# Cosine-similarity attention on one core: TensorE work cut into 64-row halves, joint operations on VectorE, four exponential chunks off ScalarE instead of two

## The chip, the cores and the metric

The kernel runs on one core of one Trainium2 chip. The metric is the device time of one execution in microseconds (us). A profile is one execution taken by the hardware profiler; its span runs from the first to the last instruction. The engines are TensorE (PE; its weight loads are listed apart as PEld), VectorE (DVE), ScalarE (ACT), GpSimd (POOL) and SyncE (SP), which here issues nearly all DMAs. Each engine works through its own list of instructions in order and waits for the others by semaphores.

## The reference

For 8 batches of 12 heads, 512 positions and 64 dimensions, in float32:

```python
Q_norm = Q / (np.linalg.norm(Q, axis=-1, keepdims=True) + 1e-10)
K_norm = K / (np.linalg.norm(K, axis=-1, keepdims=True) + 1e-10)
scores = np.einsum('bhqd,bhkd->bhqk', Q_norm, K_norm) / tau      # tau = 0.1
weights = np.exp(scores - np.max(scores, axis=-1, keepdims=True))
weights = weights / (np.sum(weights, axis=-1, keepdims=True) + 1e-10)
return np.einsum('bhqk,bhkd->bhqd', weights, V)
```

## The kernel before

The 96 heads are worked as 48 pairs `s` = 0 to 47 of two heads `h`. For each pair the kernel runs these operations; the short names are the keys that `P.add` gives them.

- `LD`, `LV`: DMA loads of Q (w = 0), K (w = 1) and V, 256 KB each (lines 318 to 325).
- `SQ`: squares of Q and K, from pair 4 on as one POOL instruction of 128x1024 (line 348); for pairs 2 and 3 two of 128x512 on POOL (line 342).
- `SSQ`, `RED`: sums of the squares. K's go through PE: eight matmuls of 64 columns against the identity, into columns 320 to 383 of an output bank (line 365), and then a reduction of 64 elements on DVE (line 372). Q's are reduced by DVE from 512 elements (line 376).
- `NEW`: reciprocal square roots by Newton steps on DVE (lines 401 to 410), done for groups of 1, 2 or 4 pairs.
- `SCL`: scaling of Q and K by them (line 434). Q on DVE; K on DVE for the pairs in `K_ON_DVE` and on POOL for the others.
- `TR`, `EVA`: eight PE transposes of 128x128 into `tps` (line 440), and the DVE copy from there to `qt` (line 455).
- `SCO`, `EXP`: for each of four chunks `c` of keys two PE matmuls with 64 rows and 512 columns, one for each head (line 552), and an exponential of 128x1024 on ACT (line 568). `scps` holds two chunks, so `SCO` of a chunk waits for the `EXP` two chunks earlier.
- A chunk in `OFF` gets its exponential as a polynomial: `SCX` on PE into `tps`, `X` on DVE (lines 502, 504), then `Y` steps on POOL and DVE (lines 509, 510).
- `VC`: V to bf16 on POOL (line 573).
- `PV`: 32 matmuls with 128 rows and 65 columns (line 585), one output bank for each head; `RCP` and `NRM` on DVE for each head apart (lines 604, 606); `ST`, the store.

Pair 0 has smaller forms of its own (`head0`), pair 47 others (`last`). The order of every engine is written out in `ORDER`: each number is the position at which `P.add` added the operation, so for one pair numbers run on. `run` turns needs between operations into semaphore waits; a wait stops its engine's whole list. On PE and ACT, needs on an operation of the same engine are dropped (lines 50 and 51), since these work in order. `HOLD` adds single waits by hand.

Where the numbers that matter below lie, with (pair, chunk): before the change 36 to 55 belong to the scores of pair 0, 83 and 85 are `TR` of pair 1, 87 is `SCO`(1,0), 89 (1,1), 91 (1,2), 93 (1,3); 132, 134, 136 and 138 are `SCO`(2,0) to (2,3); 159 and 161 are `SSQ` of pair 3 for Q and K; 203 is `SSQ` of pair 4, 246 of pair 5. POOL's list begins, in both kernels, with squares of pairs 0 to 3, `VC` of pairs 0 and 1, `SQ` of pair 4 and `SQ` of pair 5.

Of the kernel before, what the change touches and what calls it, by code (L numbers as in the profile page):

```python
# [5 lines left out]
ALU = mybir.AluOpType  # L6
# [4 lines left out]
class Op:  # L11
    def __init__(self, key, eng, kind, due, needs, emit, slot=None):
        self.key, self.eng, self.kind, self.due, self.emit = key, eng, kind, due, emit
        self.needs, self.slot = [n for n in needs if n is not None], slot
        self.own = False
        self.sem, self.val, self.inc, self.used = None, 0, 0, False
        self.start = self.end = None


class Program:  # L20
# [22 lines left out]
    def run(self):  # L43
# [3 lines left out]
        for e, ops in order.items():  # L47
            for o in ops:
                o.waits = [self.ops[n] for n in o.needs]
                if e in ("pe", "act") and not o.own:  # L50
                    o.waits = [p for p in o.waits if p.eng != e or p.slot is not None]
                for p in o.waits:
                    p.used = True
# [55 lines left out]
def bass_cosine_similarity_attention_kernel(  # L109
# [10 lines left out]
    NT = SEQ // 128  # L120
# [85 lines left out]
    slots = sorted((START + PERIOD * (s + 1) + 0.9 * PV_AT[4 * h + 3] + 0.05 + late(s), s, h) for s in range(NP - 1) for h in range(2) if s not in PV_LATER)  # L206
# [8 lines left out]
    session, attached, early = {}, {}, []  # L215
    for s, w in sorted(((s, w) for s in range(NP) for w in range(2) if on_pe(s, w)), key=lambda j: (due_red(j[0]), j)):
        at = due_red(s) + 0.3
        if s < EARLY:
            early.append((s, w))
            continue  # L220
        due, i, h = next(x for x in slots if x[0] >= at and (x[1], x[2]) not in attached)
        attached[i, h] = (s, w)
        session[s, w] = (h, due, [("PV", i, h, NT - 1)])
    before = [[("EVA", 0, 1, 0), ("EVA", 0, 1, 1)], []]
    for s, w in sorted(early):
        session[s, w] = (w, due_red(s), before[w])
        before[w] = [("RED", s, w)]
    bank_free = {}
    sequence = list(range(NP))
    for s, k in PV_LATER.items():  # L230
        sequence.remove(s)
        sequence.insert(s + k, s)
    for s in sequence:
        for h in range(2):
            bank_free[s, h] = before[h]
            before[h] = [("NRM", s, h)] + ([("RED",) + attached[s, h]] if (s, h) in attached else [])

    def head0(TF):
        for h in range(2):
# [4 lines left out]
            cast_in = qk[0][:, 1, h, :].rearrange("p (t d) -> p t d", t=NT)  # L244
# [6 lines left out]
            for w in range(2):  # L251
                src_, dst = qk[0][:, w, h, :], sq[0][:, 8 * w + 4 * h : 8 * w + 4 * h + 4, :]
# [3 lines left out]
                else:  # L256
# [12 lines left out]
                      out=qn[0][:, 0, :, h, :], in0=qk[0][:, 0, h, :].rearrange("p (t d) -> p t d", t=NT),  # L269
# [23 lines left out]
    def new(g):  # L293
        if g <= 0:
            return []
        return [("NEW", g, 7)] if direct_r(g) else [("NEW", g, 6), ("NEW", g, 7)]
# [7 lines left out]
    def last_direct(s):  # L304
        d = [g for g in NORM_ON_ACT if g > 0]
        return [("NEW", max(d), 7 if direct_r(max(d)) else 6)] if d and group[s] not in NORM_ON_ACT and s < 12 else []

    def pair(s):
# [6 lines left out]
        for w, x in ((0, Q), (1, K)):  # L315
            if s == 0:
                for h in range(2):
                    P.add(("LD", 0, w, h), "act" if w else "sp", "ldh", -1000 + h,  [],
                          lambda e, w=w, x=x, h=h: e.dma_start(out=qk[iq][:, w, h], in_=src(x, s)[:, h]), slot=f"head{w}_{h}")  # L319
                continue  # L320
            P.add(("LD", s, w), "act" if (s, w) in BY_SCALAR else "sp", "ld1" if s == 1 else "ld", s, [*([("CST", 0, i) if w else ("SCL", 0, 0, i) for i in range(2)] + [("SQ", 0, w, 0), ("SQ", 0, w, 1)] if s == R_QK else [key("SCL", s - R_QK, w), *(squares(s - R_QK, w) if s >= R_QK else [])])],
                  lambda e, w=w, x=x: e.dma_start(out=qk[iq][:, w], in_=src(x, s)),  # L322
# [6 lines left out]
        red = [[("RED", 0, w, 0), ("RED", 0, w, 1)] if s == R_SQ else [key("RED", s - R_SQ, w)] for w in range(2)]  # L329
# [3 lines left out]
        elif s in SQ_ON:  # L333
            for w, engs in enumerate(SQ_ON[s]):
                for h, eng in enumerate(engs if isinstance(engs, tuple) else (engs,)):
                    n = 1 if isinstance(engs, tuple) else 2
                    half = qk[iq][:, w, n * h : n * h + n].rearrange("p h x -> p (h x)")
                    dst = sq[iqs][:, 8 * w + 4 * h : 8 * w + 4 * h + 4 * n, :].rearrange("p g d -> p (g d)")
# [17 lines left out]
        x2 = (xs[g][:, 0 : 2 * m] if acts else n_ps[:, g % R_X, 0 : 2 * m]).rearrange("p (w x) -> p w x", w=2)  # L356
        for w in range(2):
            sqs = squares(s, w)
            dst = x2[:, w, c8 : c8 + 8]
            if (s, w) in session:  # L360
                bank, due, before = session[s, w]

                def ssq(e, w=w, bank=bank):
                    for k in range(8):
                        last = e.matmul(  # L365
                            out=o_ps[bank][:, 320:384], lhsT=ident[:, :], rhs=sq[iqs][:, 8 * w : 8 * w + 8, 8 * k : 8 * k + 8],
# [3 lines left out]
                P.add(("SSQ", s, w), "pe", "ssq", due, [*sqs, "eye"] + before, ssq)  # L370
                P.add(("RED", s, w), "dve", "redp", due + 0.1, [("SSQ", s, w), ("NRMS", 0, 0, 1), *new(g - R_X), *last_direct(s)],
                      lambda e, bank=bank, dst=dst: e.tensor_reduce(  # L372
                          out=dst, in_=o_ps[bank][:, 320:384].rearrange("p (g e) -> p g e", e=8), axis=AX.X, op=ALU.add))
            else:
                P.add(("RED", s, w), "dve", "red", due_red(s) + 0.5 * w, [*sqs, ("NRMS", 0, 0, 1), *new(g - R_X), *last_direct(s)],
                      lambda e, w=w, dst=dst: e.tensor_reduce(  # L376
                          out=dst, in_=sq[iqs][:, 8 * w : 8 * w + 8, :], axis=AX.X, op=ALU.add))
# [5 lines left out]
        on_dve = [i for i in range(first[g], first[g] + sizes[g]) if i in K_ON_DVE]  # L383
        free = [[("SCL", i, k) for i in range(first[g - R_X], first[g - R_X] + sizes[g - R_X])] if g > R_X else []
                for k in range(2)]
        reds = [("RED", i, w) for i in range(first[g], first[g] + sizes[g]) for w in range(2)]
# [13 lines left out]
        elif s == first[g]:  # L400
            yx = lambda e: e.tensor_tensor(out=tg, in0=xg, in1=yg, op=ALU.mult)  # L401
            yyx = lambda e: e.scalar_tensor_tensor(  # L402
                out=tg, in0=tg, scalar=-0.5, in1=yg, op0=ALU.mult, op1=ALU.mult)

            def up(dst, lo, hi):
                return lambda e: e.scalar_tensor_tensor(  # L406
                    out=dst, in0=tg[:, lo:hi], scalar=1.5, in1=yg[:, lo:hi], op0=ALU.add, op1=ALU.mult)
# [5 lines left out]
                yx, yyx, up(yg, 0, 2 * m), yx, yyx, up(rq_g, 0, m), up(rk_g, m, 2 * m)]  # L413
            if on_dve:
                steps.append(up(tg[:, m : 2 * m], m, 2 * m))
            for k, step in enumerate(steps):
                needs = [("NEW", g, min(k, 6) - 1 if k < 8 else 7)] if k else reds + (free[1] if K_ON_DVE else [])
                if k == 0 and g == R_X:
                    needs += [("NRMS", 0, w, h) for w in range(2) for h in range(2)]
                if 6 <= k < 8:  # L420
                    needs += free[k - 6]
                P.add(("NEW", g, k), "dve", "new", TF - 4.9 - slack(s, M_NEW) + (M_STEP * (k - 7) if s > 8 else 0.23 * k), needs, step)

        if s in off_of:
            P.add(("UNIT", s), "dve", "new", TF - 3.0, [("NEW", g, 6)], lambda e: e.tensor_scalar(
                out=rq_g[:, c8 : c8 + 8], in0=rq_g[:, c8 : c8 + 8], scalar1=UNIT * inv_tau / math.log(2.0), scalar2=1.0,
                op0=ALU.mult, op1=ALU.mult))
        for w in range(2):
            dve = w == 0 or s in K_ON_DVE
            r = (rkd[:, c8 : c8 + 8] if dve else rk_g[:, c8 : c8 + 8]) if w else rq_g[:, c8 : c8 + 8]  # L430
            r = r.rearrange("p (h t) -> p h t", h=2).unsqueeze(3).to_broadcast([128, 2, NT, DIM])
# [405 lines left out]
```

## Time and profile before

| | |
|---|---|
| device time, median of 3 runs | 188.92 us (188.57 to 189.04) |
| profiled execution | span 186.6 us; the page gives no other time of it; the median is 2.3 us above |
| busy share of the span | PE 94%, DVE 94%, ACT 97%, POOL 86% |
| DMA | 37.75 MB read, 12.58 MB written, 270 GB/s over the span |
| granted TensorE clock | 0.998 |

In the profile a group of instructions is listed with its line, engine, operation, output<-input, shapes and count, then the busy time and the mean of one in ns. A timeline row is: start, length, engine, line, operation, tiles, count, and in brackets the idle time before it with what ended it. A matmul's length holds its latency, so matmuls in a row overlap; what one costs its engine is the distance from start to start. The same holds, by a smaller amount, for DVE and ACT.

### The profile page before, as it was taken

What the parts mean: (1) busy time and instruction counts of PE and PEld (TensorE: products, weight loads), DVE (VectorE), ACT (ScalarE), POOL (GpSimd) and SP (SyncE); (2) the same over time, 40 slices, a digit from 0 to 9 for tenths busy, and PEclk for the clock granted to TensorE, in tenths of its full rate; (3) what the DMA queues carried; (4) which work ended last, traced back from release to release, by engine and by line L of the source; (5) the groups of instructions that cost most, each with busy time, mean ns of one, the idle gap of its engine ahead of it and who ended that gap; (6) DMA issues with size and microseconds to landing.
All of it is one profiled execution on the core that took longest, in us unless ns stands there. A gap on an engine that the chain in (4) does not pass through costs nothing.

```text
span 186.6 us, 6661 instructions
## 1 busy us (share of the span) xinstructions
PE 174.7 (94%) x2705; PEld 108.6 (58%) x2705; DVE 174.9 (94%) x567; ACT 181.1 (97%) x213; POOL 161.3 (86%) x148
## 2 busy tenths in 40 slices
PE   6998899999999999999999999899999999999993
PEld 2455466656666565656666565466655666555662
DVE  2799999999999999999999999999999999999863
ACT  5999999999999999999999999999999999999993
POOL 5689999999999999999999999977999999398000
PEclk9999999999999999999999999999999999999999
DMA  4999999999999999999999999999306221131535
GB/s 162 326 359 348 348 350 369 348 351 367 379 368 355 295 372 352 376 356 382 376 355 380 374 346 317 354 319 286 118 4 189 88 90 35 58 114 61 169 102 183
DMA packets 52446, 50.76 MB, mean 272 GB/s; under 512 B 3264, under 2 KB 52416, under 8 KB 52416
## 3 DMA queue, kind: packets, MB, share of 16 engines
q1 hardware_dynamic: 51984, 50.05, 80.4%
q8 instruction: 21, 0.34, 0.7%
q10 hardware_dynamic: 432, 0.30, 0.5%
q14 instruction: 9, 0.07, 0.1%
HBM read 37.75 MB, written 12.58 MB: 270 GB/s over the span
## 4 chain that ended last, share of the span: by engine, by line
ACT 88%; SPq 4%; DMA 4%; POOL 1%; DVE 1%; PE 1%; issue 0%
ACT et L568 88%; DMA qk<-in_K_dram 4%; SPq L322 2%; SPq L325 1%; POOL sq L348 1%; SPq L319 0%; DVE ob L640 0%; ACT et L563 0%; PE ops L365 0%; DVE rd L632 0%; PE scps L552 0%; PE ops L621 0%
## 5 line engine op out<-in xcount | busy, mean ns | idle before, releaser
L568 ACT ACTIVATE et<-scps 128x1024 bf16<-128x1024 f32 x185 | 170.0, 1201 | 0.2 <-PE scps L552 0.2
L348 POOL TENSOR_TENSOR sq<-qk 128x1024 bf16<-128x1024 f32 x44 | 82.6, 1892 | 1.4 <-DVE xz L510 1.3
L552 PE MATMUL scps<-qt 64*128 64x512 bf16 x372 | 72.6, 386 | 4.6 <-ACT et L568 2.4
L585 PE MATMUL ops<-vb,et 128*128 128x65 bf16 x1504 | 72.8, 194 | 0.9 <-DVE ob L606 0.4
L585 PEld LDWEIGHTS ops<-vb,et 128*128 128x128 bf16 x1504 | 55.2, 98 | 30.1 <-issue 17.8
L434 DVE TENSOR_TENSOR qn<-qk,nps 128x512 bf16<-128x512 f32 x61 | 40.4, 676 | 0.6 <-ACT nps L393 0.6
L606 DVE TENSOR_TENSOR ob<-ops,rd 128x256 f32<-128x256 f32 x94 | 38.5, 417 | 0.5
L434 POOL TENSOR_TENSOR qn<-qk,rk 128x512 bf16<-128x512 f32 x33 | 34.1, 1042 | 3.3 <-DVE rk L406 3.2
L440 PE MATMUL tps<-ident,qn 128*128 128x128 bf16 x376 | 33.3, 221 | 0.5 <-DVE qn L434 0.2
L455 DVE COPY qt<-tps 128x1024 bf16<-128x1024 bf16 x47 | 32.1, 682 | 0.2 <-PE tps L440 0.2
L376 DVE TENSOR_REDUCE nps<-sq 128x8 f32<-128x512 bf16 x46 | 30.4, 683 | 0.2
L573 POOL TENSOR_SCALAR vb<-vf 128x512 bf16<-128x512 f32 x48 | 29.2, 625 | 1.4 <-PE ops L585 1.3
L552 PEld LDWEIGHTS scps<-qt 64*128 64x128 bf16 x372 | 18.0, 93 | 21.0 <-ACT et L568 7.8
L440 PEld LDWEIGHTS tps<-ident,qn 128*128 128x128 bf16 x376 | 21.4, 98 | 13.3 <-issue 4.3
L365 PE MATMUL ops<-sq,ident 128*128 128x64 bf16 x384 | 18.9, 193 | 1.0 <-POOL sq L348 0.5
L604 DVE RECIPROCAL rd<-ops 128x4 f32<-128x4 f32 x94 | 15.5, 172 | 2.7 <-PE ops L585 2.6
L365 PEld LDWEIGHTS ops<-sq,ident 128*128 128x128 bf16 x384 | 14.2, 98 | 4.2 <-POOL sq L342 1.7
L372 DVE TENSOR_REDUCE nps<-ops 128x8 f32<-128x64 f32 x46 | 9.8, 215 | 0.0
L402 DVE SCALAR_TENSOR_TENSOR nps<-nps,ys 128x32 f32<-128x32 f32 (+2 forms) x34 | 7.0, 207 | 0.4
L401 DVE TENSOR_TENSOR nps<-nps,ys 128x32 f32<-128x32 f32 (+2 forms) x34 | 7.0, 206 | 0.4
L342 POOL TENSOR_TENSOR sq<-qk 128x512 bf16<-128x512 f32 (+1 forms) x5 | 4.7, 954 | 2.2 <-DMA qk<-in_K_dram 1.6
L192 PE MATMUL ops<-warm_in,ident 128*128 128x512 bf16 x8 | 3.6, 628 | 1.4 <-POOL eps L185 1.4
(67 smaller groups left out, 69.4 us busy)
## 6 DMA issues: line engine op xcount, KB each, us to landing
vf<-in_V_dram SPq DMA_DIRECT2D x48, 256.0 KB, 6.5
qk<-in_Q_dram SPq DMA_DIRECT2D x47, 256.0 KB, 5.6
qk<-in_K_dram SPq DMA_DIRECT2D x47, 256.0 KB, 6.6
out_dram<-ob SPq DMA_DIRECT2D x47, 256.0 KB, 5.1
qk<-in_Q_dram SPq DMA_DIRECT2D x2, 128.0 KB, 2.6
qk<-in_K_dram ACTq DMA_DIRECT2D x2, 128.0 KB, 2.8
out_dram<-ob SPq DMA_DIRECT2D x1, 128.0 KB, 1.9
out_dram<-ob SPq DMA_DIRECT2D x1, 96.0 KB, 1.7
```

The source lines that it names most:

```text
L348: lambda e: e.tensor_tensor(out=sqf, in0=data, in1=data, op=ALU.mult))
L365: last = e.matmul(out=o_ps[bank][:, 320:384], lhsT=ident[:, :], rhs=sq[iqs][:, 8 * w : 8 * w + 8, 8 * k : 8 * k + 8], start=(k == 0), stop ...
L376: lambda e, w=w, dst=dst: e.tensor_reduce(out=dst, in_=sq[iqs][:, 8 * w : 8 * w + 8, :], axis=AX.X, op=ALU.add))
L434: lambda e, w=w, r=r: e.tensor_tensor(out=qn[iqn][:, w].rearrange("p t h d -> p h t d"), in0=qk[iq][:, w].rearrange("p h (t d) -> p h t d" ...
L440: last = e.transpose(t_ps[:, w, t, :], qn[iqn][:, w, t].rearrange("p h d -> p (h d)"), ident[:, :])
L455: lambda e: e.tensor_copy(out=qt[iqt][:, :, :, :].rearrange("p w t x -> p (w t x)"), in_=t_ps[:, :, :, :].rearrange("p w t x -> p (w t x)")))
L552: last = e.matmul(out=sc_ps[:, 2 * b + h, :], lhsT=qt[iqt][64 * h : 64 * h + 64, 1, c, :], rhs=qt[iqt][64 * h : 64 * h + 64, 0, :, :], sta ...
L568: lambda e, c=c, b=b: e.activation(out=et[iet][:, c, :, :], in_=sc_ps[:, 2 * b : 2 * b + 2, :], func=ACT.Exp, scale=math.log(2.0) / UNIT i ...
L573: lambda e: e.tensor_scalar(out=vb[:, iq, :, :, 0:DIM].rearrange("p c h d -> p h c d"), in0=vf[iv][:, :, :].rearrange("p h (c d) -> p h c ...
L585: last = e.matmul(out=o_ps[h][:, 65 * t : 65 * t + 65], lhsT=et[iet][:, c, h, 128 * t : 128 * t + 128], rhs=vb[:, iq, c, h, :], start=(c = ...
L604: (lambda e, h=h, grid=grid: e.reciprocal(out=rd[io][:, h, :], in_=grid[:, :, DIM])))
L606: lambda e, h=k, grid=grid: e.tensor_tensor(out=ob[io][:, h], in0=grid[:, :, 0:DIM], in1=rd[io][:, h, :].unsqueeze(2).to_broadcast([128, N ...
```

## The change

It is one rewrite with four parts.

1. **PE in 64-row halves, from pair 4 on.** Every `PV`, `SSQ` and `TR` matmul of 128 rows becomes two of 64 rows. In `PV` and `SSQ` rows 0 to 63 and rows 64 to 127 alternate and go to different output banks: in turn 0 the lower rows work on head 0 while the upper work on head 1, in turn 1 the other way round. Turn 1 waits for the end of turn 0; such waits of PE on itself are listed in the new `hard`. Q's and K's squares are both summed on PE. `TR` runs all eight lower halves as one operation and then, after a wait, all eight upper halves. Pairs 1 to 3 and 47 keep the 128-row form.
2. **Joint operations on DVE.** One `SCL` of 128x1024 for Q and K, one `RCP` and one `NRM` for both heads, one `RED` for up to two pairs; POOL scales nothing any more. The group's Newton steps are seven, not eight or nine.
3. **Four chunks off ACT**, (15,3), (24,3), (33,3) and (42,3), all of form B (`Y` 0 to 2 on POOL, 3 and 4 on DVE), not (30,3) and (43,3).
4. **New orders** for all engines, other `GROUPS` and `HOLD`. The layout of `qk` changes from [Q/K][head] to [head][Q/K].

```diff
+    def phase(i, turn):
+        return bank_half[i] if turn else [("PV", i, 0, 0)]
...
+                def sums(e, turn=turn):
+                    for k in range(8):
+                        for r in (0, 1):
+                            h = r ^ turn
+                            last = e.matmul(
+                                out=o_ps[h][:, at : at + 64], lhsT=ident[64 * r : 64 * r + 64, :],
+                                rhs=sq[iqs][64 * r : 64 * r + 64, 8 * h : 8 * h + 8, 8 * k : 8 * k + 8],
+                                start=False, stop=(turn == 1 and k == 7), skip_group_check=True)
+                    return last
+
+                P.add(("SSQ", s, turn), "pe", "ssqh", due_red(s), [("SQ", s, 0), "eye"] + phase(i, turn), sums).hard = phase(i, turn) if turn else []
...
+            P.add(("SCL", s), "dve", "sclj", T0 - 2.55 - slack(s, M_SCL), [("NEW", g, 6)] + gone,
...
+            def half(e, r=w):
+                rows = slice(64 * r, 64 * r + 64)
+                for w in range(2):
+                    for t in range(NT):
+                        last = e.transpose(
+                            t_ps[:, w, t, rows], qn[iqn][rows, w, t].rearrange("p h d -> p (h d)"), ident[rows, rows])
+                return last
...
+        for turn in (0, 1):
+            for c in range(NT):
+                def pv(e, c=c, turn=turn):
+                    for t in range(NT):
+                        for r in (0, 1):
+                            h = r ^ turn
+                            last = e.matmul(
+                                out=o_ps[h][:, 65 * t : 65 * t + 65],
+                                lhsT=et[iet][64 * r : 64 * r + 64, c, h, 128 * t : 128 * t + 128], rhs=vb[64 * r : 64 * r + 64, iq, c, h, :],
+                                start=(turn == 0 and c == 0 and t == 0), stop=(turn == 1 and c == NT - 1), skip_group_check=True)
                     return last
...
+        P.add(("RCP", s), "dve", "rcpj", T0 + 2 * PERIOD, bank_full[s] + [key("NRM", s - R_O)],
...
-OFF = {(30,3):((30,30),'B'),(43,3):((43,43),'A')}
+OFF = {(15,3):((15,15),'B'),(24,3):((24,24),'B'),(33,3):((33,33),'B'),(42,3):((42,42),'B')}
-GROUPS = [1, 1, 1, 1, 2, 2, 2, 2, 2, 2, 2, 2, 4]
+GROUPS = [1, 1, 1, 1, 1, 2, 2, 2, 2, 4]
...
     "pe": (
-        "6 24 22 -256 38 44 48 36 76 78 40 46 52 114 50 42 116 83 85 54 159 87 161 89 57 58 59 91 128 130 93 63 60 "
-        "64 132 203 65 134 66 246 136 172 174 138 176 102 178 103 104 105 280 180 215 217 182 96 97 98 219 147 99 "
...
+        "6 24 22 -256 38 44 48 36 74 76 40 46 52 110 50 112 42 151 153 81 83 54 85 57 87 191 59 58 89 122 124 60 91 229 "
+        "126 64 230 61 62 63 192 128 163 165 130 94 132 96 97 266 95 167 267 100 99 98 101 169 202 171 203 135 173 136 "
```

In the new PE list 151 and 153 are `SSQ` of pair 3 for Q and K, 81 and 83 `TR` of pair 1, 54 the scores of the last chunk of pair 0, 85, 87, 89 and 91 `SCO`(1,0) to (1,3), 57 to 64 `PV` of pair 0 (turn 0: 57 to 60), 191 and 192 `SSQ` of pair 4, 229 and 230 of pair 5, 122 and 124 `TR` of pair 2, 126 and 128 `SCO`(2,0) and (2,1).

More of the change, by code (lines that the diff above doesn't have):

```diff
@@ L214, in bass_cosine_similarity_attention_kernel @@
         users.sort()
[L215 to L228, printed above, removed]
     sequence = list(range(NP))
@@ L382, in pair @@
         rkd = n_ps[:, g % R_X, 128 + m : 128 + 2 * m] if acts else tg[:, m : 2 * m]
[L383 to L386, printed above, removed]
+        free = [scl(i, k) for i in range(first[g - R_X], first[g - R_X] + sizes[g - R_X]) for k in range(2)] if g > R_X else []
+        reds = [("RED", i, *w) for i in range(first[g], first[g] + sizes[g]) for w in (((0,), (1,)) if i < EARLY else ((),)) if i < EARLY or i in red_of]
         if s == first[g] and g in NORM_ON_ACT:
@@ L672 @@
 JOINT = ()
-PV_LATER = {30:1}
+PV_LATER = {15:1,24:1,33:1,42:1}
 TURNED = range(0)
```

225 lines of the change are left out of this document (125 added, 100 removed), and 146 rows, old and new, of the table ORDER.

## The prediction

> **What bounds the kernel now.** I read the page's busy shares first, then the chain of waits that ended last, then the groups by line, and last the timelines of the head (6 to 20 us) and of a steady stretch. From the page and, for L502 and L510, from the groups with shapes kept apart:
>
> ```profile
> PE 174.7 (94%) x2705; PEld 108.6 (58%) x2705; DVE 174.9 (94%) x567; ACT 181.1 (97%) x213; POOL 161.3 (86%) x148
> ACT 88%; SPq 4%; DMA 4%; POOL 1%; DVE 1%; PE 1%; issue 0%
> L568 ACT ACTIVATE et<-scps 128x1024 bf16<-128x1024 f32 x185 | 170.0, 1201 | 0.2 <-PE scps L552 0.2
> L434 DVE TENSOR_TENSOR qn<-qk,nps 128x512 bf16<-128x512 f32 x61 | 40.4, 676 | 0.6 <-ACT nps L393 0.6
> L606 DVE TENSOR_TENSOR ob<-ops,rd 128x256 f32<-128x256 f32 x94 | 38.5, 417 | 0.5
> L434 POOL TENSOR_TENSOR qn<-qk,rk 128x512 bf16<-128x512 f32 x33 | 34.1, 1042 | 3.3 <-DVE rk L406 3.2
> L376 DVE TENSOR_REDUCE nps<-sq 128x8 f32<-128x512 bf16 x46 | 30.4, 683 | 0.2
> L455 DVE COPY qt<-tps 128x1024 bf16<-128x1024 bf16 x47 | 32.1, 682 | 0.2 <-PE tps L440 0.2
> L604 DVE RECIPROCAL rd<-ops 128x4 f32<-128x4 f32 x94 | 15.5, 172 | 2.7 <-PE ops L585 2.6
> L372 DVE TENSOR_REDUCE nps<-ops 128x8 f32<-128x64 f32 x46 | 9.8, 215 | 0.0
> L401 DVE TENSOR_TENSOR nps<-nps,ys 128x32 f32<-128x32 f32 (+2 forms) x34 | 7.0, 206 | 0.4
> L502 DVE TENSOR_SCALAR xp<-tps 128x512 int16<-128x512 f32 x4 | 2.7, 678 | 0.0
> L510 DVE SCALAR_TENSOR_TENSOR xz<-xz,xp 128x1024 f32<-128x1024 f32 x1 | 1.2, 1219 | 0.0
> ```
>
> PE and DVE look as full as ACT, but the chain is ACT's for 88%: its exponentials follow each other to the end. These rows give the pace, from the chain and from ACT's timeline in three windows:
>
> ```profile
> 15.32 1.90 POOL sq L348
> 18.04 164.34 ACT et L568 x179
> ...
> 85.95 2.94 ACT L568 ACTIVATE et<-scps 128x1024 bf16<-128x1024 f32 x3
> ...
> 98.60 3.11 ACT L568 ACTIVATE et<-scps 128x1024 bf16<-128x1024 f32 x3
> ...
> 181.96 1.47 ACT L563 ACTIVATE et<-scps 128x512 bf16<-128x512 f32 x3
> ```
>
> From 85.95 to 98.60 lie 14 chunks: 0.904 us each, a pair of four 3.62 us. From 18.04 to 181.96 the 179 chunks take 163.9 us where 179 x 0.904 is 161.8: **2.1 us are lost in small delays** of ACT. PE's steady timeline shows why:
>
> ```profile
> 100.26 0.40 PE L440 MATMUL tps<-ident,qn 128*128 128x128 bf16 x4
> 100.49 0.41 PE L585 MATMUL ops<-vb,et 128*128 128x65 bf16 x8
> 100.85 0.39 PE L552 MATMUL scps<-qt 64*128 64x512 bf16 x2
> 101.18 0.66 PE L585 MATMUL ops<-vb,et 128*128 128x65 bf16 x16
> 101.67 0.40 PE L365 MATMUL ops<-sq,ident 128*128 128x64 bf16 x8
> 102.00 0.39 PE L552 MATMUL scps<-qt 64*128 64x512 bf16 x2
> ...
> 6.49 0.60 PE L541 MATMUL scps<-qt 64*128 64x512 bf16 x2 [0.18 <-DVE qt L290]
> ```
>
> Matmuls for values start 0.031 us apart (16 in 0.49, from 101.18 to 101.67), sums about 0.03, transposes 0.058 (four in 0.23). Two score matmuls in the same 64 rows (L541) take 0.60, so one streams for 0.60 - 0.39 = 0.21. The two of L552, in different halves, take 0.39 together: **the halves run at the same time.** After them the next work starts not 0.21 but 0.33 later (100.85 to 101.18), and before them the last sum starts at 101.67 + 0.40 - 0.19 = 101.88, with the scores at 102.00 instead of 101.91. Each change of form costs about 0.1 us, eight changes a pair 0.8. PE's pair: scores 4 x 0.21, values 32 x 0.031, transposes 8 x 0.058, sums 8 x 0.03, changes 0.8, together 3.3 of 3.62 us. That leaves little; the chunk between 100.85 and 102.00 holds 1.15 us of PE work for 0.904 of ACT.
>
> **The change, part by part.**
>
> *Two more chunks off ACT.* 2 x 0.904 = **-1.8 us**, all on the chain.
>
> *PE in halves.* From pair 4 on nothing changes form. If alternating halves run like L552's, two of them cost one place: values 32 x 0.031, sums 16 x 0.03 (Q's are new), transposes 16 x 0.03 (64 columns, not 128, one half after the other), scores 0.84: 2.8 us a pair. A wait of PE for its own last matmul, 0.2 us (L365's length less a place), stands open where nothing lies between the turns, about once a pair, with the rest of the values and the next scores behind it; elsewhere scores or transposes lie between. So 3.0 us, and a chunk with four value operations and a sum is 24 x 0.03 + 0.21 = 0.93, against 1.15 above. This frees up to all of the 2.1 us (bounds 0 and -2.1, and a loss if halves do not pair up, below). I take half, **-1.0**, because DVE stays nearly full.
>
> *DVE.* Its timeline shows how much sooner than its length an instruction is followed:
>
> ```profile
> 105.16 0.68 DVE L434 TENSOR_TENSOR qn<-qk,nps 128x512 bf16<-128x512 f32 x1
> 105.75 0.18 DVE L604 RECIPROCAL rd<-ops 128x4 f32<-128x4 f32 x1
> 105.85 0.66 DVE L434 TENSOR_TENSOR qn<-qk,nps 128x512 bf16<-128x512 f32 x1
> ```
>
> By some 0.08 to 0.09: 676 ns cost 0.60. Before: L376 46 x 0.60, 42 of L372 x 0.13, L604 94 x 0.09, L606 94 x 0.34, L434 61 x 0.60. After: `SCL` 44 x 1.14 (L510's 1024 elements) and 6 x 0.60 (+17), `RED` 21 of 256 elements at 0.33 and two at 0.20 (-26), `RCP` 47 x 0.10 (-4), `NRM` 47 x 0.61 (-3), 37 fewer Newton steps and unit scalings at 0.12 (-4, by L401), four polynomials of 4 x 0.60 + 2 x 1.14 = 4.7 for two of 4.7 and 4.2 (+10). Sum -10 of about 170. Yet between pairs 13 and 42 a pair is 1.14 + 0.17 + 0.10 + 0.61 + 0.60 (L455) + 0.21 (Newton) = 2.83, and 30 x 2.83 + 19 = 104 us stand against ACT's 116 x 0.904 = 105: as full as before, hence only half of the delays.
>
> *POOL.* Loses 34 us of scaling, gains some 9 of polynomials; its squares run ahead of their use from pair 6 on, and I cost it at nothing. Without that cover DVE would stand at `Y` 3 for one POOL step, 1.9 us (15.32, as many elements), with copies for the next scores behind it: four times, 7.6 us at most. The new layout of `qk` keeps a load's runs at 256 floats, as the source has them: nothing, hidden behind the other loads of the queue.
>
> *The head.* Here the new order has a price. The timelines of POOL, ACT and PE before:
>
> ```profile
> 10.06 2.04 POOL L342 TENSOR_TENSOR sq<-qk 128x512 bf16<-128x512 f32 x2 [0.44 <-DMA qk<-in_Q_dram]
> 13.36 3.86 POOL L348 TENSOR_TENSOR sq<-qk 128x1024 bf16<-128x1024 f32 x2
> ...
> 8.76 3.56 ACT L544 ACTIVATE et<-scps,xs 128x512 bf16<-128x512 f32 x6
> 12.18 5.62 ACT L568 ACTIVATE et<-scps 128x1024 bf16<-128x1024 f32 x6
> 18.04 3.85 ACT L568 ACTIVATE et<-scps 128x1024 bf16<-128x1024 f32 x4 [0.24 <-PE scps L552]
> ...
> 10.05 0.68 PE L440 MATMUL tps<-ident,qn 128*128 128x128 bf16 x8
> 11.56 0.39 PE L552 MATMUL scps<-qt 64*128 64x512 bf16 x2
> 12.15 0.41 PE L365 MATMUL ops<-sq,ident 128*128 128x64 bf16 x8 [0.20 <-POOL sq L342]
> 17.61 0.39 PE L552 MATMUL scps<-qt 64*128 64x512 bf16 x2
> ```
>
> POOL's list and the loads up to pair 5 stay as they are, so pair 3's K squares end at 12.10, pair 4's at 15.25, pair 5's at 17.22, as now. Operation 153 (sums of 3, K) now stands ahead of `TR`(1), the last scores of pair 0 and `SCO`(1,0). It starts at 12.15, as the row shows; 8 x 0.03 gives 12.39, eight transposes 12.85, a change of form 12.95 for the scores of pair 0, and ACT follows 0.43 later (17.61 to 18.04) at 13.4 instead of 11.6 (8.76 + 5 x 0.57). `EVA`(1), behind the transposes' end at 13.0, takes 0.7 on DVE; `SCO`(1,0) goes at 13.75 instead of 11.56, `EXP`(1,0) at **14.2 instead of 12.18**. Next, 191 (sums of 4) stands ahead of `SCO`(1,2): 15.30, a sum operation 0.24, two of values 0.25, scores at 15.8, `EXP`(1,2) at **16.2 instead of 14.0**; not a second loss but the same one seen again. 229 (sums of 5) is ready at 17.27, with `EXP`(2,0) due at 18.1: in time. Between `SCO`(2,0) and (2,1) lie 32 places, 1.0 us, which makes `EXP`(2,1) 19.2, 0.2 late. From `EXP`(2,2), 20.1 against 18.04 (which holds the 0.24 of idle), ACT's pace decides up to pair 4, and nothing later gives it back, since ACT is full. **+2.0 us**; bounds 0 (if squares come sooner) and 2.7 (if the halves go singly: sum 0.47, values 0.5).
>
> *Tail.* Pair 47 keeps its forms; the joint `NRM` of 46 (0.7 us) ends before the last exponential: nothing.
>
> *Sum.* Span 186.6 - 1.8 - 1.0 + 2.0 = 185.8; the median lies 2.3 above the span: **188.0** (-0.5%). Own range: all delays gone 187.0, none gone and 0.2 more 189.3.
>
> **Rivals.**
>
> *Halves go singly (slower).* L552 shows two long matmuls side by side, but no row shows many short ones fed in a row; the closest, L585, needs a load and a matmul each 0.031 us. If that is the rate of the feed, PE's pair is 64 x 0.031 + 32 x 0.03 + 16 x 0.03 + 0.84 = 4.3, 0.65 over ACT's 3.62, for 43 pairs 28 us: about 216. At 0.04 for two places PE needs 3.4 with its waits, and it decides from about 0.044 for two; at 0.05 it is 3.9 and +12: 201; at 0.047, 195. The Trainium skill, page "TensorE: Matmul & The Clock Gate", section "Wait — 56ns, not 53.3ns?", has a floor of about 25 ns from start to start however small a matmul; by it, as an estimate, 112 short matmuls take 2.8 us and the pair 3.65 before waits, which is this rival at its mild end. L552's two, a few ns apart in a joint 0.39, speak against that floor across halves. For it: the feed of PE doubles, 240 loads and matmuls in 3.62 us. I give 0.27.
>
> *PE's relief buys nothing.* DVE sets the small delays, and the joint operations of 1.14 us hold up copies: 2.1 stays, 189.0 to 190. DVE's 94% speaks for it, the crowded chunk at 100.85 against. 0.14.
>
> *The head loses nothing.* 186.0 to 187.0, if loads of pairs 3 and 4 land 2 us sooner. The 0.44 us that POOL waited for Q at 10.06 says the transfers set it, and their order is unchanged. 0.07.
>
> *The change does not do what it says:* pairing fails to remove the changes of form, since transposes write 64 columns. Then PE needs 3.6 or more and it is the second rival again; its chance is within that.
>
> **How the numbers follow.** The forecast has 0.52: of it 0.38 faster by over 0.3% (under 188.35), 0.12 within, 0.02 slower. 0.3% is about what a measurement of this kernel can tell from no change. Head without loss 0.07, faster. PE's relief nothing: 0.06 within, 0.08 slower. Halves singly: 0.27 slower, half of it under 196. Together 0.45, 0.18, 0.37. The range 186.8 to 195 leaves out some 0.04 below and 0.15 above; the likeliest case alone is 187.0 to 189.3.
>
> **What would show it.** Right: ACT's first 128x1024 exponential near 14.2 with PE waiting for POOL's squares at 12.1 and 15.3; value matmuls in pairs a few ns apart, 0.03 from pair to pair; no gap of 0.1 around L552's successors; ACT at 0.904 in long stretches. Wrong: PE without idle and ACT waiting for scores in every pair (the halves go singly), an early start of pair 1, or DVE named before most late scores.

## The result and the profile after

| | before | after |
|---|---|---|
| device time, median | 188.75 us (188.42 to 189.04) | 230.99 us (228.55 to 235.05) |
| ratio | | 1.219 (95%: 1.213 to 1.226) |
| span of the profiled execution | 186.6 us | 228.8 us |
| granted TensorE clock | 0.998 | 0.921 |

Ratios rest on the fast runs alone: some executions of one program run some per cent longer, and the profiled execution of sums_turns_full (217.41 us), little_traffic (210.63) and before_split64_few (198.26) was such a slow one.

The change costs 42 us. The forecast was 188.0 us, the range ended at 195: direction and size were wrong. From the page of the changed kernel (busy rows, clock in 40 slices, DMA queues, chain, groups):

```profile
PE 178.0 (78%) x5633; PEld 129.8 (57%) x5633; DVE 170.2 (74%) x372; ACT 185.3 (81%) x211; POOL 137.3 (60%) x120
PEclk9958775979799999999979997999999999998898
q8 instruction: 44, 0.72, 1.4%
PE 47%; ACT 21%; issue 14%; DVE 11%; DMA 3%; SPq 1%; POOL 1%
L623 ACT ACTIVATE et<-scps 128x1024 bf16<-128x1024 f32 x183 | 173.8, 1041 | 35.5 <-PE scps L607 34.6
```

Of the page before, the one row that matters beside the prediction's is the queue that carries instructions:

```profile
q8 instruction: 21, 0.34, 0.7%
```

No engine is full any more. ACT waits 35.5 us ahead of its large exponentials (0.2 before), for scores; PE is busy for 78% only, and a new word stands in the chain with 14%: "issue", time in which an engine waited for nothing that the profile shows. The waits say where (us in all, times, longest):

```profile
ACT et L623 <- PE scps L607: 34.6, 38, 3.1
...
PEld ops L641 <- issue: 26.4, 37, 3.0
...
PE ops L641 <- issue: 18.0, 13, 2.9
```

PE's timeline in a steady stretch shows two such stops:

```profile
100.65 0.54 PE L641 MATMUL ops<-vb,et 64*128 64x65 bf16 x24
101.01 0.42 PE L397 MATMUL ops<-sq,ident 64*128 64x64 bf16 x16
101.24 0.31 PE L641 MATMUL ops<-vb,et 64*128 64x65 bf16 x8
101.36 0.40 PE L607 MATMUL scps<-qt 64*128 64x512 bf16 x2
101.61 0.39 PE L641 MATMUL ops<-vb,et 64*128 64x65 bf16 x13
103.55 0.46 PE L641 MATMUL ops<-vb,et 64*128 64x65 bf16 x19 [1.55 <-issue]
...
107.85 0.44 PE L641 MATMUL ops<-vb,et 64*128 64x65 bf16 x17 [1.00 <-issue]
```

PE stops in the middle of the values, between matmuls that have nothing to wait for. Where becomes plain when PE's records (loads, matmuls and PE's few waits) are numbered in order of their starts. These are the 16 longest pauses from start to start in the trace between 14 us and the last 300 records, by their number modulo 256:

```
changed kernel   193 in all 16 (numbers 705, 961, 1217, 1473, 1985, ... 8129); 1.09 to 3.10 us
kernel before    54 94 99 253 194 114 220 198 151 4 224 112 152 78 92 181; 0.42 to 0.91 us
```

The list of PE comes in blocks of 256: queue q8 moved 0.72 MB in 44 packets, 16 KB each, and 44 x 256 is 11,264, about the 11,266 loads and matmuls of the busy row. Each packet's start and end can be set beside the start of the block in the trace:

```
changed kernel, block that starts at        25.96   33.26   39.95   45.06
packet of the block after it starts         30.73   37.39   42.64   47.57
... and has landed                          31.86   38.50   43.84   48.53
that block's first instruction starts       33.26   39.95   45.06   49.98
pause ahead of it                            3.10    1.18    1.99    0.06
```

In the changed kernel no packet starts before the block ahead of it has begun, as if the next block were asked for at that moment (the request itself is in no trace). Where a pause follows, the packet starts 0.95 to 4.8 us after that beginning, takes some 1.1, and the first instruction runs 1.2 to 1.6 us after it has landed. That loop lasts 3.7 to 7.3 us, while PE works through a block, without the pause at its end, in 2.6 us at the least and in under 3.8 half the time. Before the change a block lasted some 8 us, so the same loop was hidden. **The pauses at block starts, each less 0.1 us, sum to 32.4 us; before to 0.0.** I call this theory F, the feed. Of the 34.6 us that ACT waits for scores, 29.6 lie beside such a pause of over 0.25 us: they overlap it or begin within 1.5 us of its end.

The ledger on ACT: the large exponentials start at 12.18 us before the change and at 15.12 after it; the shorter exponentials behind them start at 181.96 and at 224.09. Of the 42.2 us by which the span grew, 2.9 lie in the head (below), 35.3 are more idle time ahead of the large exponentials, and two chunks fewer give 1.8 back. The rest, 5.8 us, is ACT's pace outside these stops: (224.09 - 15.12 - 35.3) / 183 = 0.949 us a chunk, where the kernel before has (181.96 - 12.18 - 0.2) / 185 = 0.917, its small delays included. The window with little data traffic lies between the two:

```profile
170.05 32.64 ACT L623 ACTIVATE et<-scps 128x1024 bf16<-128x1024 f32 x35 [1.58 <-PE scps L607]
203.13 8.36 ACT L623 ACTIVATE et<-scps 128x1024 bf16<-128x1024 f32 x9 [0.45 <-PE scps L607]
...
224.09 1.28 ACT L618 ACTIVATE et<-scps 128x512 bf16<-128x512 f32 x3
```

35 chunks from 170.05 to 203.13, less 0.45 of idle, are 0.932 us each.

### The profile page after: what moved, and what is told of

The parts are those of the page before. It is cut to its first block, busy times and chain, and to the rows that moved or that the text cites. A ratio compares the mean times of both kernels' runs of the same rounds, so it can differ in the third digit from the quotient of the medians.

```text
span 228.8 us, 12319 instructions
## 1 busy us (share of the span) xinstructions
PE 178.0 (78%) x5633; PEld 129.8 (57%) x5633; DVE 170.2 (74%) x372; ACT 185.3 (81%) x211; POOL 137.3 (60%) x120
## 4 chain that ended last, share of the span: by engine, by line
PE 47%; ACT 21%; issue 14%; DVE 11%; DMA 3%; SPq 1%; POOL 1%
ACT et L623 21%; PE ops L641 20%; PE scps L607 13%; PE ops L397 8%; PE tps L500 5%; DVE ob L653 5%; DMA qk<-in_Q_dram 3%; DVE nps L409 1%; DVE qt L510 1%; DVE rd L651 1%; DVE xz L559 1%; PE tps L492 1%; SPq L352 1%; POOL sq L373 1%; DVE xp L557 1%
## 5 line engine op out<-in xcount | busy, mean ns | idle before, releaser
L623 ACT ACTIVATE et<-scps 128x1024 bf16<-128x1024 f32 x183 | 173.8, 1041 | 35.5 <-PE scps L607 34.6
L641 PE MATMUL ops<-vb,et 64*128 64x65 bf16 x3008 | 87.7, 196 | 25.8 <-issue 18.0
L641 PEld LDWEIGHTS ops<-vb,et 64*128 64x128 bf16 x3008 | 69.9, 98 | 45.9 <-issue 26.4
L607 PE MATMUL scps<-qt 64*128 64x512 bf16 x368 | 82.7, 411 | 9.7 <-ACT et L623 5.0
L478 DVE TENSOR_TENSOR qn<-qk,nps 128x1024 bf16<-128x1024 f32 x44 | 53.0, 1213 | 0.2
L397 PE MATMUL ops<-sq,ident 64*128 64x64 bf16 x1408 | 39.7, 195 | 4.4 <-issue 4.4
L500 PE MATMUL tps<-ident,qn 64*128 64x64 bf16 x704 | 38.0, 197 | 3.1 <-issue 1.8
L500 PEld LDWEIGHTS tps<-ident,qn 64*128 64x128 bf16 x704 | 30.4, 99 | 13.1 <-PE tps L500 4.3
L397 PEld LDWEIGHTS ops<-sq,ident 64*128 64x128 bf16 x1408 | 31.4, 98 | 8.9 <-issue 6.6
L651 DVE RECIPROCAL rd<-ops 128x8 f32<-128x8 f32 x47 | 9.7, 205 | 35.3 <-PE ops L641 26.0
L653 DVE TENSOR_TENSOR ob<-ops,rd 128x512 f32<-128x512 f32 x47 | 32.2, 686 | 0.5
```

The lines of the kernel that those rows point to most:

```text
L397: last = e.matmul(out=o_ps[h][:, at : at + 64], lhsT=ident[64 * r : 64 * r + 64, :], rhs=sq[iqs][64 * r : 64 * r + 64, 8 * h : 8 * h + 8, ...
L478: lambda e: e.tensor_tensor(out=qn[iqn][:, :].rearrange("p w t h d -> p h (w t) d"), in0=qk[iq][:, :].rearrange("p h w (t d) -> p h (w t) ...
L500: last = e.transpose(t_ps[:, w, t, rows], qn[iqn][rows, w, t].rearrange("p h d -> p (h d)"), ident[rows, rows])
L607: last = e.matmul(out=sc_ps[:, 2 * b + h, :], lhsT=qt[iqt][64 * h : 64 * h + 64, 1, c, :], rhs=qt[iqt][64 * h : 64 * h + 64, 0, :, :], sta ...
L623: lambda e, c=c, b=b: e.activation(out=et[iet][:, c, :, :], in_=sc_ps[:, 2 * b : 2 * b + 2, :], func=ACT.Exp, scale=math.log(2.0) / UNIT i ...
L641: last = e.matmul(out=o_ps[h][:, 65 * t : 65 * t + 65], lhsT=et[iet][64 * r : 64 * r + 64, c, h, 128 * t : 128 * t + 128], rhs=vb[64 * r : ...
```

## The experiments

Each kernel is the changed one or the one before with one edit. "Pauses" are those at block starts, from the second block on, in the profiled run.

| kernel | loads and matmuls on PE | fetches | pauses, us | median, us | ratio to before |
|---|---|---|---|---|---|
| before | 5,410 | 21 | 0.0 | 188.75 | |
| changed | 11,266 | 44 | 32.4 | 230.99 | 1.219 (1.213 to 1.226) |
| full_rows | 6,146 | 24 | 0.0 | 202.95 | 1.078 (1.068 to 1.089) |
| values_full | 8,258 | 32 | 2.2 | 217.23 | 1.154 (1.138 to 1.169) |
| sums_turns_full | 9,154 | 36 | 8.7 | 215.11 | |
| few_loads | 11,266 | 44 | 13.4 | 208.7 | 1.109 (1.102 to 1.115) |
| little_traffic | 11,266 | 44 | 15.6 | 207.07 | 1.087 (1.082 to 1.092) |
| window3 | 11,266 | 44 | 5.7 | 258.26 | 1.366 (1.357 to 1.375) |
| before_split64 | 10,618 | 41 | 23.5 | 219.55 | 1.162 (1.154 to 1.170) |
| before_split128 | 7,642 | 30 | 6.2 | 194.42 | 1.019 (1.008 to 1.030) |
| before_split64_few | 10,618 | 41 | 5.8 | 197.18 | 1.034 (1.026 to 1.042) |

### Back to 128 rows: full_rows, values_full, sums_turns_full

```diff
-                    for t in range(NT):
-                        for r in (0, 1):
-                            h = r ^ turn
+                    for t in (2 * turn, 2 * turn + 1):
+                        for h in (0, 1):
...
-                                lhsT=et[iet][64 * r : 64 * r + 64, c, h, 128 * t : 128 * t + 128], rhs=vb[64 * r : 64 * r + 64, iq, c, h, :],
+                                lhsT=et[iet][:, c, h, 128 * t : 128 * t + 128], rhs=vb[:, iq, c, h, :],
```

This is the edit of values_full. sums_turns_full does the like to `SSQ` and `TR` alone, full_rows all of it; for `SSQ`:

```diff
-                        for r in (0, 1):
-                            h = r ^ turn
...
-                                out=o_ps[h][:, at : at + 64], lhsT=ident[64 * r : 64 * r + 64, :],
+                            out=o_ps[turn][:, at : at + 64], lhsT=ident[:, :],
```

> The changed kernel with values, sums and transposes back in 128-row form (one matmul where two halves stood), the two waits of TensorE on itself dropped, and everything else (orders, joint VectorE operations, four chunks off ScalarE) as changed. Theory F (TensorE's instructions come in blocks of 256 by DMA; the next block is asked for when the one before begins and is usable 5 to 7 us later while loads run, but the halves use up a block in about 4 us): 128 instructions a pair, a block lasts about 7.2 us, so the gaps at every 256th instruction vanish (under 1 us in all) and the time is 189 to 194 us. Theory O (the new orders, the joint operations and the turns cost the time): 220 us or more, with late scores as in the changed kernel.

> Only the values go back to 128 rows; sums and transposes stay in halves. 176 instructions a pair, a block lasts 5.3 us at ScalarE's pace. F: gaps at block boundaries shrink to a third or less of the changed kernel's 32 us, all of them while loads run; 196 to 206 us. O: no change from 229, or more, since changes of form come back.

> Only sums and transposes go back to 128 rows; values stay in halves. 192 instructions a pair, a block lasts 4.8 us. F: between values_full and the changed kernel, 203 to 216 us. O: about 229.

Measured: full_rows 202.95 us, values_full 217.23, sums_turns_full 215.11. From full_rows' page:

```profile
PE 186.1 (92%) x3073; PEld 120.8 (60%) x3073; DVE 170.2 (84%) x372; ACT 186.5 (92%) x211; POOL 137.2 (68%) x120
q8 instruction: 24, 0.39, 0.8%
PE 68%; DVE 13%; ACT 10%; DMA 3%; issue 2%; SPq 2%; POOL 1%
```

With the same orders, joint operations and four chunks off ACT, but half the instructions, the pauses are gone and 28 us with them. That refutes orders and joint operations as the main cause. It is not the 189 to 194 that F expected: PE in whole rows, with Q's sums added, is itself the chain (68%) and full. How much of the 14 us above the kernel before is Q's sums and how much the orders, these runs don't separate. The two mixed forms do not bear F out: values_full has 2.2 us of pauses and still loses 29 us, and sums_turns_full meets its range with 8.7 us of pauses in a loss of some 27, so by luck. In both PE is the largest part of the chain again (67% and 56%). They change between whole and half rows within a pair; that this costs the time is likely, but no run shows it.

### Less data traffic: few_loads, little_traffic

```diff
+    def rows(s, ring):
+        return 128 if s < ring else 32
...
-                  lambda e, w=w, x=x: e.dma_start(out=qk[iq][:, :, w], in_=src(x, s)),
+                  lambda e, w=w, x=x: e.dma_start(out=qk[iq][0:rows(s, R_QK), :, w], in_=src(x, s)[0:rows(s, R_QK)]),
```

`LV` is cut in the same way; PE's list is the changed kernel's. little_traffic cuts the stores as well:

```diff
-              lambda e: e.dma_start(out=src(out, s), in_=ob[io][:, :].rearrange("p h t d -> p h (t d)")), slot=f"out{io}")
+              lambda e: e.dma_start(out=src(out, s)[0:32], in_=ob[io][0:32].rearrange("p h t d -> p h (t d)")), slot=f"out{io}")
```

> The changed kernel, but loads of Q and K from pair 17 on and of V from pair 9 on bring only 32 of the 128 partitions (the rest of a slot keeps older data, so the output is not the reference's). All instructions stay. F: blocks arrive sooner when few loads are queued, so from the point where the full loads have landed (about 30 us) the gaps fall below 0.5 us each; 192 to 205 us. O, or a cost of the halves themselves: 225 us or more.

> few_loads with stores of 32 of 128 partitions as well (pairs 0 to 46): the output is written in part only, and Q and K from pair 17 on and V from pair 9 on are loaded in part only. All PE instructions, orders and other work are those of the changed kernel. F: gaps at every 256th instruction nearly gone from 45 us on, 3-8 us in all (few_loads 13.4), time 196-204 against few_loads' 208.7, ACT at 0.905-0.925 a chunk from 60 us on. O: the orders and the joint operations hold the time at 207 or more although the traffic is gone.

few_loads took 208.7 us, 22 less than the changed kernel with every instruction kept, but above the 205 at which F's expectation ended; F also had each pause under 0.5 us from some 30 us on, and after 50 us some still last up to 1.8. Late in it ACT hardly stops:

```profile
144.69 57.35 ACT L626 ACTIVATE et<-scps 128x1024 bf16<-128x1024 f32 x62 [0.30 <-PE scps L610]
```

little_traffic, 207.07, missed F's 196 to 204, and its pauses, 15.6 us, the 3 to 8 expected. 8.3 of them end by 42 us, where the full loads of the first 17 pairs still run, which the edit leaves alone; 7.2 come later, with little traffic. From 60 us on its packets start about 1.0 us after the block ahead has begun, and yet the loops that end in a pause last 3.6 to 4.5 us: about the 3.62 x 256 / 240 = 3.9 us in which ACT wants 256 instructions. Less traffic shortens the loop, but not by enough to hide it.

### Traffic throttled or paced: window3, before_window3, paced5

```diff
+        for j, o in enumerate(order["sp"]):
+            if j >= 14:
+                o.waits = o.waits + [order["sp"][j - 3]]
```

This is the edit of window3 and before_window3. paced5 has:

```diff
+    for s in range(13, NP):
+        for w in range(2):
+            P.ops["LD", s, w].needs.append(("SQ", s - 5, 0))
```

> The changed kernel with one edit: from its 15th on, each DMA that SP issues first waits for the landing of the one three places earlier, so that at most three of these transfers are under way; Q's and K's loads get semaphores of their own. PE's work and all orders are unchanged. F (the blocks of 256 PE instructions come late because their fetch queues behind data transfers): the wait from the request to the first packet falls from 2-4.8 us to under 2 us, the gaps at every 256th PE instruction fall from 32 us in all to under 15, the time to 200-215. O (orders and joint operations set the time) and C (the halves themselves, or the clock alone): PE's work, the orders and DVE's operations are the same, so 228-235, and the gaps stay or are a symptom of something else. A loss from the waits of SP themselves would show as ACT or POOL waiting for DMA.

> The kernel before with the same limit of three transfers under way: a control. F: its blocks of 256 arrive in time anyway (gaps 0.015 us in all), so 188-190 by all theories; more shows what the limit itself costs.

> The changed kernel with one edit: from pair 13 on the loads of Q and K of pair s also wait for POOL's squares of pair s-5, so that loads are issued at the pace of use and not as soon as a slot of the ring of 17 is free; the bytes are the same. F (instruction fetches queue behind data): the median from issue to landing of the data falls from about 6 us to 3-4.5, the delay of the fetches falls with it, the gaps at every 256th PE instruction fall from 32 us to 8-20, and the time to 205-222, faster than the changed kernel's 231. O and C (orders, joint operations, halves' own cost): no effect or a loss, 229-240.

window3 brought the pauses from 32.4 to 5.7 us and the longest delay of a packet with a pause behind it from 4.8 to 2.0, as F has it; but the time rose to 258.26, and the same limit costs the kernel before 52 us (240.52; 1.274, 1.268 to 1.280). The waits of window3 show the price:

```profile
ACT et L626 <- PE scps L610: 62.3, 39, 11.6
POOL vb L631 <- DMA vf<-in_V_dram: 38.9, 11, 6.8
```

POOL now waits for V: three transfers of 256 KB under way, 3.5 us each from issue to landing, are 0.22 MB a us, where the kernel before moves 0.27. The gap between the two kernels shrank from 42 to 18 us, but the limit is no remedy. paced5 took 239.12 (234.80 to 240.07), where F had 205 to 222. Its median delay of a packet stayed at 1.8 us (2.0 in the changed kernel), its pauses at 26.6, while POOL now waits 9.1 us for V and 6.2 for K. It says little on F, as what it should have changed hardly changed.

### A longer list alone: before_nops, before_waits, before_split64 and its kin

```diff
+                        for _ in range(4):
+                            e.wait_ge(P.ops["eye"].sem, 1)
                     return last
```

In before_waits this stands behind each matmul of a `PV` operation (eight operations of four matmuls a pair); the trace has two wait instructions there, 64 a pair. In before_nops the added line is `e.nop(nofuse=True)`.

> The kernel before with four no-operations behind each matmul operation's group for values (16 groups a pair of the two heads' chunks, each of its four matmuls followed by four no-operations or as the list has them: 128 more PE instructions a pair, in all about as many as the changed kernel has). Matmuls, forms, orders, all other engines unchanged. F: gaps appear at every 256th PE instruction and the time rises to 205-225, with ACT waiting for the scores behind them. C (halves) and O (orders, joint operations): nothing that they name is in it, so 188-190; if the no-operations cost PE time by themselves, the delay is spread evenly and shows no period of 256.

> The kernel before with four waits that are long met behind each of PE's operations for values (16 such operations a pair: 64 instructions more on PE, some 3,000 in all, PE's list 1.55 times as long). Matmuls, their forms, all orders and all other engines as before. (before_nops turned out to add nothing: the no-operations are in no trace and the number of instruction fetches stayed 21.) F: about 33 fetches instead of 21, gaps at every 256th instruction of PE's list once a block lasts less than the fetch loop of 5-7 us, 3-20 us in all, above all before 140 us, with a period of 256 in PE's list, counted with the added ones. Rival S (a met wait costs PE itself 0.015 us or more: 64 x 0.015 = 1 us a pair): delays spread over every operation, ACT's pace at 1.0 a chunk or more also after 140 us where the DMA queues are quiet.

Neither told anything of F. before_nops took 188.70 (1.000, 0.999 to 1.002) because the no-operations are not in the program that ran: its page has 21 fetches, as before. before_waits took 425.12: its 3,008 more wait instructions cost 236 us, 0.079 us each, spread over the values, as rival S said; the granted clock, 0.60, is part of that. A block lasts 12 us there, so F has no pauses to show. What was needed were instructions that cost PE nothing else, and the score matmuls can be cut into such:

```diff
-                for h in range(2):
+                for x in range(0, SEQ, 64):
+                    for h in range(2):
...
-                        rhs=qt[iqt][64 * h : 64 * h + 64, 0, :, :], start=True, stop=True)
+                            rhs=qt[iqt][64 * h : 64 * h + 64, 0, x // 128, x % 128 : x % 128 + 64],
+                            start=True, stop=True, skip_group_check=True)
```

> The kernel before with one edit: each score matmul of 512 columns becomes eight of 64, the two heads (rows 0 to 63 and 64 to 127) by turns. Same weights, same columns, same results; 112 more loads and matmuls a pair, some 5,200 in all, so that PE's list is about as long as the changed kernel's (42 fetches instead of 21). Values, sums, transposes, all orders, all other engines as before. By the changed kernel's rows two pieces of 64 columns take 0.029 us, a chunk's eight 0.23 instead of 0.21 us, 0.1 us a pair. F (a PE list twice as long comes late): gaps at every 256th PE instruction, 15-45 us in all, 205-230, ACT waiting for the scores behind them. H (not the length of the list but the halves of values, sums and transposes, or the orders and joint operations of the changed kernel): 188.5-195, no period of 256. S (the pieces cost PE more by themselves): delays in every chunk, also after 150 us.

> The same in four pieces of 128 columns: 48 more instructions a pair, some 2,200 in all, about 30 fetches. F: a block then lasts about 5.6 us against a fetch loop of 5-7.3: gaps of 0-10 us in all, 188.5-198, clearly less than before_split64. H: as before_split64, 188.5-191.

> before_split64 with loads of only 32 of 128 partitions for Q and K from pair 17 on and for V from pair 9 on (so most values of later pairs are computed from older data); PE's list is that of before_split64. F: gaps small from 70 us on, 4-15 us in all, 10-25 us faster than before_split64. S: the pieces' own cost does not depend on the traffic: within 3 us of before_split64.

All three fell where F put them: 219.55, 194.42 and 197.18 us. PE's timeline in before_split64, around one pause:

```profile
40.43 0.41 PE L553 MATMUL scps<-qt 64*128 64x64 bf16 x16
40.77 0.39 PE L587 MATMUL ops<-vb,et 128*128 128x65 bf16 x7
43.33 0.64 PE L587 MATMUL ops<-vb,et 128*128 128x65 bf16 x9 [2.17 <-issue]
43.91 0.61 PE L553 MATMUL scps<-qt 64*128 64x64 bf16 x16
44.45 0.62 PE L587 MATMUL ops<-vb,et 128*128 128x65 bf16 x8
```

The stop again cuts a row of 16 value matmuls in two (7 and 9), inside an operation of four, at record 1473, again 193 modulo 256, as are all of its 16 longest. And with the traffic cut (before_split64_few), ACT's timeline:

```profile
46.79 145.22 ACT L573 ACTIVATE et<-scps 128x1024 bf16<-128x1024 f32 x158 [0.48 <-PE scps L556]
191.70 1.36 ACT L568 ACTIVATE et<-scps 128x512 bf16<-128x512 f32 x3
```

158 chunks in 144.91 us, 0.917 each, with the long list: no more than the kernel before needs with the short one (0.917), so the pieces themselves cost next to nothing, and 22 of the 31 us that before_split64 loses go when the data traffic is cut. So a longer PE list, in a kernel where nothing but the cut of the score matmuls is changed, gives the pauses; half the dose (30 fetches) gives a quarter of them, at a granted clock of 1.00, so they don't come from a lower clock. This settles the main cause.

### The head: full_head

```diff
-112 42 151 153 81 83 54 85 57 87 191 59 58 89 122 124 60 91 229 126
+112 42 81 83 54 151 85 153 87 57 59 58 89 122 124 60 91 126 191 128 229
```

This is the head of PE's order in full_rows (later places and DVE's list are moved alike).

> full_rows with the head's order undone by hand: the sums of pair 3 stand behind the transposes of pair 1 and the last scores of pair 0, those of pair 4 and 5 behind the scores of pair 1, and DVE's copies of pair 1 ahead of its reductions of pair 3. H (the order of the head costs about 2 us for good): the first 128x1024 exponential at 12-12.6 instead of about 15, and 200.5-201.5 where full_rows has 202.95. Rival (the late start is made good later, since PE sets the pace there and not ACT): the first exponential is sooner, the time is the same within 0.6.

Its ACT timeline:

```profile
12.83 2.85 ACT L621 ACTIVATE et<-scps 128x1024 bf16<-128x1024 f32 x3 [0.16 <-PE scps L605]
16.84 3.04 ACT L621 ACTIVATE et<-scps 128x1024 bf16<-128x1024 f32 x3 [1.16 <-PE scps L605]
20.79 2.86 ACT L621 ACTIVATE et<-scps 128x1024 bf16<-128x1024 f32 x3 [0.90 <-PE scps L605]
24.89 2.18 ACT L621 ACTIVATE et<-scps 128x1024 bf16<-128x1024 f32 x2 [1.25 <-PE scps L605]
27.62 1.03 ACT L621 ACTIVATE et<-scps 128x1024 bf16<-128x1024 f32 x1 [0.54 <-PE scps L605]
28.89 16.64 ACT L621 ACTIVATE et<-scps 128x1024 bf16<-128x1024 f32 x16 [0.25 <-PE scps L605]
```

The same stretch of the changed kernel, ACT and then PE:

```profile
14.26 0.69 ACT L599 ACTIVATE et<-scps,xs 128x512 bf16<-128x512 f32 x1 [2.21 <-PE scps L596]
15.12 2.96 ACT L623 ACTIVATE et<-scps 128x1024 bf16<-128x1024 f32 x3 [0.17 <-PE scps L607]
18.78 5.60 ACT L623 ACTIVATE et<-scps 128x1024 bf16<-128x1024 f32 x6 [0.70 <-PE scps L607]
```

```profile
12.64 1.04 PE L492 MATMUL tps<-ident,qn 128*128 128x128 bf16 x8
13.61 0.61 PE L596 MATMUL scps<-qt 64*128 64x512 bf16 x1
```

The first large exponential came 1.8 us sooner than full_rows' 14.62, yet the time was 204.86 (1.087, 1.083 to 1.090), not less than full_rows' 202.95. H's 200.5 to 201.5 is refuted for this order, but the rival's "same within 0.6" is not met either: by 28.89 us ACT has stopped five times for scores, 4.1 us in all, where full_rows stops for 1.3 us up to 20.87 and then runs through 24 chunks. The order made by hand loses again what it gains. Whether a late start by itself is given back later stays open.

No experiment points to a version that beats both kernels: in its quiet stretch the changed kernel's ACT pace is still 0.932, against 0.917 before, and the one edit that nearly cures the pauses and keeps the bytes (window3) costs more than they do.

## Why the prediction was wrong, point by point

- **What bounds before** was read rightly: ACT's exponentials, PE close behind.
- **PE in halves**, the failed step. "If alternating halves run like L552's, two of them cost one place ... So 3.0 us": the places are right. 24 value matmuls take 0.36 us (100.65 to 101.01), 0.030 for two; 16 sums take 0.23, 0.029 for two; transposes follow each other by 0.029, with 0.25 between the lower and the upper halves; and after scores the next work starts 0.25 us later, not 0.33, so that changes of form are nearly gone. But the sum had only PE's places in it, and the supply of the list was costed at nothing. Its cover before was the 8 us that a block lasts; the change takes it away, with 240 loads and matmuls a pair. That term is 32.4 us of pauses.
- **The relief of ACT, -1.0**, did not come. Outside the pauses ACT's pace is 0.949 instead of 0.917, and even in the quiet stretch it is 0.932. What makes these 0.015 to 0.03 us was not tried and stays open.
- **Two chunks off ACT, -1.8**: 183 instead of 185 large exponentials, as said; invisible beside the rest.
- **DVE and POOL** show little of it: DVE's busy time fell from 174.9 to 170.2 us, and of the 35.5 us that ACT waits ahead of its large exponentials PE's scores end 34.6, most of them beside a block's pause.
- **The head, +2.0**: the mechanism was right, `EXP`(1,0) at 15.12 where 14.2 was forecast and 12.18 stood before. The 0.9 beyond goes with PE's lower clock there (0.72 from 8 to 20 us, 1.00 before): eight transposes take 1.04 us instead of 0.68, a score matmul 0.61 instead of 0.39. That it is never given back was not tested: full_head makes losses of its own.
- **The rival "halves go singly"** came nearest to the time (195 to 216) by another mechanism, and the trace refutes it: two halves do cost one place. Its remark that the feed of PE doubles held the answer, but it looked for a steady rate per matmul, not for a block of 256 that comes late. The queue row q8 in the page of before, with 21 packets of 16 KB, could have asked the question: how long is the way of the next block, and how long does this one last?
- **The sum** slips by 0.1: 185.8 + 2.3 is 188.1.

A rule of the Trainium skill speaks to this term, and the prediction did not weigh it. Its page "Runtime: NRT & Kernel Launch", section "Instruction fetch mechanics", has the next 16 KB fetched while the current block runs, and holds that the fetch is hidden, since instructions are issued more slowly than they arrive. The trace agrees with the first (a packet starts after each block's begin) and not with the second: in the changed kernel 256 instructions can run in 2.6 us, and where a pause follows their successors take 3.7 to 7.3.

## What to carry to other kernels

Count the instructions of an engine, not only its busy time: an edit that splits matmuls doubles the list, and a list is fetched in blocks that must last longer than the way of the next one. Here that means 256 instructions in no less than 5 to 7 us under full data traffic and some 4 us in quiet. "issue" stops between instructions that wait for nothing, at a fixed period in the engine's list, are the sign.

## What the runs showed of the hardware that was not expected

- One block of 256 PE instructions is under way at a time: each of the changed kernel's 44 packets starts after the block ahead has begun and before the next one does. The delay depends on the other DMA traffic (packet start about 1.0 us after that beginning in little_traffic from 60 us on, up to 4.8 in the changed kernel between 20 and 40 us, at a DMA share of 1.10).
- Behind a long pause PE's clock was lower. In before_split64 16 score pieces took 0.34 us before the pause (40.43 to 40.77) and 0.54 after it (43.91 to 44.45). In windows of the changed kernel (busy times, then granted clock, DMA share, GB/s):

```profile
8.00:20.00 12.00, 10.23 (x194) 6.59 (x195) 7.96 (x28) 8.91 (x16) 11.61 (x11) 0.72 1.10 351
20.00:40.00 20.00, 13.60 (x387) 10.62 (x381) 11.23 (x32) 12.37 (x13) 15.17 (x11) 0.74 1.10 352
...
180.00:200.00 20.00, 18.62 (x664) 13.58 (x664) 18.89 (x36) 20.00 (x23) 8.23 (x7) 1.00 0.26 83
```

  The clock is 0.74 from 20 to 40 us, with the longest pause (3.1 us), and 1.00 where the DMA share is 0.26 and ACT is busy for all 20 us. That it is 0.72 already from 8 to 20 us, ahead of the first pause, stays unexplained.
- Wait instructions between matmuls, for a semaphore met long before, cost 0.079 us of the kernel's time each (236 us for 3,008 in before_waits, at a granted clock of 0.60 instead of 1.00).
